# A decoder layer on one core: the remaining transposes, those of the softmax among them, through VectorE blocks and DRAM, and attention five steps earlier

## Chip, cores and metric

One core of a Trainium2 chip runs the whole layer. The metric is device time in microseconds: three runs of the kernel before gave 2067.03 to 2070.13 us, median 2067.54. TensorE is PE in the rows, VectorE DVE, ScalarE ACT, GpSimd POOL, and SyncE SP, whose queue issues all DMAs here.

## What is computed

A layer over 256 positions of width 2048, all float32:

```
x = x + 1/2 * SwiGLU_1(rms(x))                      # D_FF 5632
h = rms(x);  q|k|v|u|v_sg|g_att|g_sg = h @ w_in     # 12 heads of 128 in 3 groups, u and v_sg 1536 wide
y_att = (attention of the 3 groups, weighted by their softmax denominators) @ w_att_out
y_sg  = (gelu(u) * (tril(sg_w) @ LN(gelu(v_sg)) + sg_b)) @ w_sg_out
x = x + (sigmoid(g_att) * y_att + sigmoid(g_sg) * y_sg) @ w_out
x = x + 1/2 * SwiGLU_2(rms(x));  out = rms(x)
```

The three groups have dilations 1, 4 and 16. Attention works on four slots; a slot is one head of each group, and its softmax runs over the three groups at once (1152 columns of scores for 128 rows: 384 for the first row block, 768 for the second).

## The kernel before

Each weight gemm makes 512 output columns for both row blocks of 128 positions. Its weights come as units of four k-tiles (512 rows x 512 columns, 1 MiB, tile `raw`, three buffers). A unit has two *steps*; a step is two k-tiles. For a step, ScalarE rounds the weights to `wh` (L131) and VectorE makes the rest `wl` (L132), and TensorE does 12 matmuls (L146 to L148: hi x wh, hi x wl, lo x wh, for two k-tiles and two row blocks). Splits are issued `LA` = 3 steps ahead of the products, into four buffers. All 776 steps stand in one list `hus` in the order of the calls of `gemm`; the loop at the end (L747 on) goes through it, issues the products of a step, then the callbacks that `at(i, fn)` put at it, then the loads and splits that are due. Nothing else sets the order of work. Each engine takes its instructions in that order, and SP's queue too.

The left operand of a gemm must lie transposed (model dimension on partitions), in two parts hi and lo. There are two ways to turn it. Either TensorE transposes 128x128 pieces into a bank of the tag `tp`, and ScalarE and VectorE empty it; or `turn` (L158): at step i VectorE transposes 32x32 blocks (L165) into `bt` and SP writes it to DRAM (`bm`, L168, 512 KB); at step i+3 SP reads it back in four parts of 32 partitions (L174); at step i+6 ScalarE and VectorE make hi and lo. The h of both feed-forward blocks, q and k, c = 0 to 2 of the two inner norms and c = 0 to 2 of the merge go through `turn`. TensorE still transposes: x for the first norm while it is loaded, c = 3 of the norms (`norm_transposes`, L208) and of the merge (L612), the spatial weights (L343), the gated u (L421), the softmax (L519, L522) and the attention output (L555).

A feed-forward block runs in two halves of 6 and 5 column blocks of h. The gate and up gemms have 8 steps each, a down gemm 12 steps in the first half and 10 in the second; four down gemms follow each half. The last h of a half is turned while the first down gemm runs. Its callbacks, with e the last step of the up gemm: multiply e+1, blocks e+2, read e+5, evacuation e+8; the first down gemm reaches that h at step e+9 of the second half (e+11 of the first).

Mixer: v_sg, u, then q and k of each group, then v, then four times (gate of the spatial branch, `w_sg_out`, gate of attention, `w_att_out`), then `w_out`. `spatial(e)` puts its product, gate, transposes and evacuation for six pairs of groups at steps e to e+8. `attention(e)` puts slot s at e0 = e + 5s: scores e0, softmax e0+1, transposes e0+3, evacuation e0+4, p@v e0+5, normalisation, transposes and evacuation of the output up to e0+8.

Of the kernel before, what the change touches and what calls it, by code (L numbers as in the profile page):

```python
# [8 lines left out]
F32 = mybir.dt.float32  # L9
# [3 lines left out]
OP = mybir.AluOpType  # L13
# [28 lines left out]
def layer(ctx: ExitStack, tc: tile.TileContext, a, out):  # L42
# [58 lines left out]
    def gemm(w, c0, rows0, nk, lhs, post, before=None):  # L101
        g = dict(w=w, c0=c0, rows0=rows0, nk=nk, lhs=lhs, post=post)
        gemms.append(g)
        for u in range(nk // UK):
            for j in range(2):
                hus.append((g, u, j))
# [51 lines left out]
    def turn(i, name, src, dst, ev):  # L158
        got = {}

        def blocks():
            d = sb.tile([P, 4, 4, NT, 32], F32, tag="gate", bufs=2, name=f"bt{name}")
            v = src()
            for t in range(NT):
                DVE.transpose(d.rearrange("p j k t b -> p t k j b")[:, t],  # L165
                              v[:, t].rearrange("p (k j b) -> p k j b", j=4, b=32))
            m = got["m"] = dram.tile([P, 4, S], F32, tag="turn", name=f"bm{name}")
            SP.dma_start(m, d.rearrange("p j k t b -> p j (k t b)"))  # L168

        def back():  # L170
            got["e"] = e = dst()
            m = got["m"].rearrange("(i a) j r -> j a i r", a=32)
            for j in range(4):
                SP.dma_start(e[32 * j:32 * j + 32].rearrange("p t c -> p (t c)").rearrange("p (i r) -> p i r", i=4),  # L174
                             m[j])

        at(i, blocks)
        at(i + 3, back)
        at(i + 6, lambda: ev(got["e"].rearrange("p t c -> p (t c)").rearrange("p (i q b) -> p q i b", i=4, b=32)))

    def turned(ap):
        return ap.rearrange("p k (t i b) -> p (k t) i b", t=NT, b=32)

# [34 lines left out]
    def residual(e, n, c, banks, scale, norm):  # L218
# [14 lines left out]
        if c < 3:  # L233
            def evac(src):
                for j in range(4):
                    v = src[:, 2 * j:2 * j + 2]
                    k = 16 * n + 4 * c + j
                    ACT.activation(v, v, AF.Copy, scale=gcols[:, k:k + 1])
                ks = slice(4 * c, 4 * c + 4)
                split_psum(turned(xT["hi"][:, ks]), turned(xT["lo"][:, ks]), src)  # L240

            turn(e + 2, f"x{n}_{c}", lambda: x[:, :, cs],
                 lambda: sb.tile([P, NT, NC], F32, tag="gate", bufs=2, name=f"xt{n}_{c}"), evac)
            return
        got = {}

        def tr():
            for kk in range(2):
                ks = [4 * c + 2 * kk, 4 * c + 2 * kk + 1]
                got[kk] = ks, norm_transposes(f"{n}_{ks[0]}", ks)  # L250
            if c == 3:
                norm_rstd(n)

        def ev():
            for kk in range(2):
                norm_evac(n, *got[kk])

        at(e + 2, tr)
        at(e + 3, ev)


    def ffn(wg, wu, wd, down_post):
        halves = ((0, 6), (6, 11))
        for hf, (f0, f1) in enumerate(halves):
# [8 lines left out]
            for f in range(f0, f1):  # L273
# [10 lines left out]
                def post_up(e, banks, st=st, f=f, f0=f0):  # L284
# [17 lines left out]
                    turn(e + 2, f"h{e}", lambda: sg, lambda: sg, ev)  # L302

                gemm(wg, f * NC, 0, KD, lhs_x, post_gate)
                gemm(wu, f * NC, 0, KD, lhs_x, post_up)
            for c in range(4):
                gemm(wd, c * NC, f0 * NC, 4 * (f1 - f0), lhs_h,
                     lambda e, banks, c=c, hf=hf: down_post(e, c, banks, hf == 1))
# [5 lines left out]
    ffn(a["ffn1_w_gate"][0], a["ffn1_w_up"][0], a["ffn1_w_down"][0], down1)  # L314
# [12 lines left out]
    def mixer_consts():  # L327
        SP.dma_start(cs_t, a["rope_cs"])
        SP.dma_start(mask, a["att_mask"])
        raw = big.tile([P, NG, P], F32, tag="C", name="sgw")  # L330
        SP.dma_start(raw, a["sg_w"][0].rearrange("g t s -> t g s"))
        mix["sgraw"] = raw
# [7 lines left out]
    def sgw_transposes(q):  # L340
        b = tp_bank(f"sgw{q}").rearrange("p (j s) -> p j s", j=4)
        for j in range(4):
            PE.transpose(b[:, j], mix["sgraw"][:, 4 * q + j], ident)  # L343
        mix["sgwb", q] = b

    def sgw_evac(q):
        ACT.activation(mix["wspT"][:, 4 * q:4 * q + 4], mix["sgwb", q], AF.Copy)
        if q == 2:
            POOL.affine_select(mix["wspT"], mix["wspT"], pattern=[[0, NG], [1, P]], compare_op=OP.is_ge,
                               fill=0.0, base=0, channel_multiplier=-1)  # L350
# [44 lines left out]
    def spatial(e):  # L395
        for pg in range(6):
# [19 lines left out]
            def tr(pg=pg, got=got):  # L416
                b = tp_bank(f"spt{pg}").rearrange("p (j s) -> p j s", j=2)
                for j in range(2):
                    g = 2 * pg + j
                    for t in range(NT):  # L420
                        PE.transpose(b[:, j, t * P:(t + 1) * P], mix["u"][:, t, g * P:(g + 1) * P], ident)  # L421
                got["t"] = b

            def ev(pg=pg, got=got):
                g = slice(2 * pg, 2 * pg + 2)
                split_psum(mix["uT"][:, 0, g], mix["uT"][:, 1, g], got["t"])

            at(e + pg, prod)
            at(e + pg + 1, gate)
            at(e + pg + 2, tr)  # L430
            at(e + pg + 3, ev)

    def post_qk(key, gi):
        def post(e, banks):
# [5 lines left out]
            def flat(v):  # L440
# [370 lines left out]
```

## Time and profile before

| | |
|---|---|
| median of three runs | 2067.54 us (2067.03 to 2070.13) |
| the profiled execution | 2066.57 us, its span 2064.8 us |
| granted TensorE clock | 0.999 |
| TensorE busy, loading weights | 99%, 87% |
| VectorE, ScalarE, GpSimd busy | 56%, 47%, 0% |
| DMA | 455 MB, the dynamic queue's packets 68.1% of 16 engines' span |

A row of a view groups instructions by source line and tile; `out<-in` names the tiles. "Idle before" is the time for which the engine stood still ahead of an instruction, and the name behind it is what ended that. A matmul's own duration overlaps the next one's; how fast TensorE goes is read from the starts.

### The profile page before, as it was taken

The page shows a single profiled execution, that of the slowest core. Times are in us where ns is not written, and L with a number is a line of the kernel's source. Part 1 is how long each engine was busy: PE and PEld are TensorE (multiplying, and loading weights), DVE is VectorE, ACT ScalarE, POOL GpSimd, SP SyncE. Part 2 cuts the span into 40 slices and gives each one's busy share as a digit, 9 for nine tenths or more (in the row PEclk, how much of TensorE's full clock was granted, in tenths as well). Part 3 has the DMA queues.
Part 4 walks back from the last instruction along what each step waited for, and adds up shares of the span by engine and source line. Part 5 has one row for each costly group of instructions (what it writes and reads, how often), then busy time and mean ns, then how long its engine had stood idle before and what let it go on. Part 6 is the DMA issues. An engine that isn't in the chain of part 4 may idle for free.

```text
span 2064.8 us, 23874 instructions
## 1 busy us (share of the span) xinstructions
PE 2051.4 (99%) x9601; PEld 1794.1 (87%) x9601; DVE 1164.2 (56%) x1172; ACT 970.8 (47%) x1071; POOL 9.4 (0%) x13
## 2 busy tenths in 40 slices
PE   9999999999999999999999999999999999999998
PEld 7888888888888888888888888888888888888887
DVE  5555555455555555665555555665555555555554
ACT  6444444444445544444455444554444444444443
POOL 0000000000000000000000000000000000000000
PEclk9999999999999999999999999999999999999999
DMA  7777776677786666578646666676677766677764
GB/s 266 234 234 224 224 224 204 204 223 225 243 277 225 224 204 204 192 245 260 200 143 207 223 221 206 222 246 223 223 233 233 223 202 202 222 224 242 234 209 142
DMA packets 237399, 455.20 MB, mean 220 GB/s; under 512 B 9644, under 2 KB 32360, under 8 KB 237160
## 3 DMA queue, kind: packets, MB, share of 16 engines
q1 hardware_dynamic: 237288, 453.68, 68.1%
q8 instruction: 75, 1.23, 0.2%
q14 instruction: 36, 0.29, 0.0%
HBM read 432.14 MB, written 21.50 MB: 220 GB/s over the span
## 4 chain that ended last, share of the span: by engine, by line
PE 98%; DMA 1%; DVE 0%; issue 0%; ACT 0%; SPq 0%; ACTq 0%; POOLq 0%; POOL 0%; DVEq 0%
PE mm L148 32%; PE mm L147 32%; PE mm L146 32%; DMA bmh<-bth 0%; DMA raw<-in_ffn_w_gate_dram 0%; PE sc L495 0%; PE sp L405 0%; DMA sg<-bmh 0%; ACT wh L131 0%; PE pv L543 0%; PE pv L542 0%; PE pv L538 0%; PE sc L493 0%; PE spt L421 0%; PE pt L522 0%
## 5 line engine op out<-in xcount | busy, mean ns | idle before, releaser
L132 DVE TENSOR_TENSOR wl<-raw,wh 128x1024 fp32r<-128x1024 f32 (+1 forms) x777 | 948.6, 1223 | 855.9 <-ACT wh L131 851.3
L131 ACT ACTIVATE wh<-raw 128x1024 fp32r<-128x1024 f32 (+1 forms) x777 | 817.8, 1055 | 1023.1 <-PE mm L148 1013.0
L146 PE MATMUL mm<-wh,xhi 128*128 128x512 f32 x2144 | 815.9, 381 | 0.0
L147 PE MATMUL mm<-wl,xhi 128*128 128x512 f32 x2144 | 813.1, 379 | 0.7 <-DVE wl L132 0.7
L148 PE MATMUL mm<-wh,xlo 128*128 128x512 f32 x2144 | 812.6, 379 | 0.0
L147 PEld LDWEIGHTS mm<-wl,xhi 128*128 128x128 f32 x2144 | 405.2, 189 | 58.9 <-DVE wl L132 1.8
L148 PEld LDWEIGHTS mm<-wh,xlo 128*128 128x128 f32 x2144 | 405.2, 189 | 57.3
L146 PEld LDWEIGHTS mm<-wh,xhi 128*128 128x128 f32 x2144 | 405.2, 189 | 57.1
L148 PE MATMUL mm<-wh,hlo 128*128 128x512 f32 x704 | 267.0, 379 | 1.1 <-DVE hlo L154 1.1
L146 PE MATMUL mm<-wh,hhi 128*128 128x512 f32 x704 | 267.1, 379 | 0.0
L147 PE MATMUL mm<-wl,hhi 128*128 128x512 f32 x704 | 266.8, 379 | 0.0
L148 PEld LDWEIGHTS mm<-wh,hlo 128*128 128x128 f32 x704 | 133.1, 189 | 20.8 <-DVE hlo L154 1.9
L146 PEld LDWEIGHTS mm<-wh,hhi 128*128 128x128 f32 x704 | 133.1, 189 | 18.9 <-ACT hhi L153 0.2
L147 PEld LDWEIGHTS mm<-wl,hhi 128*128 128x128 f32 x704 | 133.1, 189 | 18.8
L146 PE MATMUL mm<-wh,mhi 128*128 128x512 f32 x128 | 48.6, 380 | 0.0
L147 PE MATMUL mm<-wl,mhi 128*128 128x512 f32 x128 | 48.5, 379 | 0.0
L148 PE MATMUL mm<-wh,mlo 128*128 128x512 f32 x128 | 48.5, 379 | 0.0
L146 PE MATMUL mm<-wh,uT 128*128 128x512 f32 x96 | 36.7, 383 | 0.0
L147 PE MATMUL mm<-wl,uT 128*128 128x512 f32 x96 | 36.4, 379 | 0.0
L148 PE MATMUL mm<-wh,uT 128*128 128x512 f32 x96 | 36.4, 379 | 0.0
L294 DVE SCALAR_TENSOR_TENSOR sg<-mm,rstd,sg 128x512 f32<-128x512 f32 x44 | 30.9, 744 | 0.0
L194 ACT ACTIVATE junk<-x 128x512 bf16<-128x512 f32 x30 | 18.9, 629 | 21.9 <-DVE x L223 15.7
(144 smaller groups left out, 644.1 us busy)
## 6 DMA issues: line engine op xcount, KB each, us to landing
raw<-in_w_in_dram SPq DMA_DIRECT2D x92, 1024.0 KB, 5.0
raw<-in_ffn_w_up_dram SPq DMA_DIRECT2D x88, 1024.0 KB, 5.2
raw<-in_ffn_w_down_dram SPq DMA_DIRECT2D x88, 1024.0 KB, 5.0
raw<-in_ffn_w_gate_dram SPq DMA_DIRECT2D x85, 1024.0 KB, 5.1
raw<-in_w_out_dram SPq DMA_DIRECT2D x16, 1024.0 KB, 5.2
raw<-in_w_sg_out_dram SPq DMA_DIRECT2D x12, 1024.0 KB, 5.5
bmh<-bth SPq DMA_DIRECT2D x22, 512.0 KB, 3.3
sg<-bmh SPq DMA_DIRECT2D x88, 128.0 KB, 4.9
```

The lines of the kernel that those rows point to most:

```text
L131: ACT.activation(wh[:, k], r[:, k], AF.Copy)
L132: DVE.tensor_tensor(wl[:, k], r[:, k], wh[:, k].bitcast(F32), op=OP.subtract)
L146: PE.matmul(o, hi[:, k, tt], in_turn(wh[:, jj]), start=first, stop=False)
L147: PE.matmul(o, hi[:, k, tt], in_turn(wl[:, jj]), start=False, stop=False)
L148: PE.matmul(o, lo[:, k, tt], in_turn(wh[:, jj]), start=False, stop=last)
L194: ACT.activation(junk, x[:, t, c * NC:(c + 1) * NC], AF.Square, accum_out=ss[n][:, t, c:c + 1])
L294: DVE.scalar_tensor_tensor(two(sg[:, t]), banks[t], rstd[:, t:t + 1], two(sg[:, t]), op0=OP.mult, op1=OP.mult)
```

## The change

It takes the last transposes in the middle of the program from TensorE and gives them to `turn`, which is made general: `put` fills the blocks (`put_tokens` for a token-major tile, `put_flat` for columns as they lie), and q 32-column blocks a row are moved.

- Norms 1 and 2: c = 3 goes through `turn` too; c = 1 begins four steps later (e+6).
- Merge: c = 3 goes through `turn`.
- Spatial weights: two turns of six groups each, 30 and 22 steps ahead of the end of the first feed-forward block, in a tile `room` of 4096 columns that takes the place of `sgw`.
- Spatial branch: three turns of four groups each, blocks at e+3, e+5, e+7, read back into `room`.
- Softmax: one turn of 1152 columns a slot, blocks e0+3, read e0+6, evacuation e0+9, so p@v is at e0+10 and the output's evacuation at e0+13. `attention` is called with e+16 in place of e+21.
- Pairs: two neighbouring gemms can be laid out so that all units but the last of both come first, then the last of the first, then the last of the second. Paired are the first two down gemms of each half, the first two of v_sg, of `w_out`, and the first gate and up of the second feed-forward block.

```diff
-    def gemm(w, c0, rows0, nk, lhs, post, before=None):
...
+    def gemm(w, c0, rows0, nk, lhs, post, pair=False):
+        gemms.append(dict(w=w, c0=c0, rows0=rows0, nk=nk, lhs=lhs, post=post, pair=pair))
+    def lay_out():
+        i = 0
+        while i < len(gemms):
+            gs = gemms[i:i + 2] if gemms[i]["pair"] else gemms[i:i + 1]
+            i += len(gs)
+            units = [(g, u) for g in gs for u in range(g["nk"] // UK)]
+            if len(gs) == 2:
+                units.sort(key=lambda q: q[1] == q[0]["nk"] // UK - 1)
+            for g, u in units:
+                hus.extend([(g, u, 0), (g, u, 1)])
...
-    def turn(i, name, src, dst, ev):
+    def turn(i, name, q, put, dst, ev):
         def blocks():
-            d = sb.tile([P, 4, 4, NT, 32], F32, tag="gate", bufs=2, name=f"bt{name}")
...
+            d = sb.tile([P, 4, q, 32], F32, tag="gate", bufs=2, name=f"bt{name}")
+            put(d)
+            m = got["m"] = dram.tile([P, 4, q * 32], F32, tag="turn", name=f"bm{name}")
+            SP.dma_start(m, d.rearrange("p j m b -> p j (m b)"))
...
+    def put_tokens(src):
+        def put(d):
+            v = src()
+            for t in range(NT):
+                DVE.transpose(d.rearrange("p j (k t) b -> p t k j b", t=NT)[:, t],
+                              v[:, t].rearrange("p (k j b) -> p k j b", j=4, b=32))
+        return put
+    def put_flat(src):
+        def put(d):
+            DVE.transpose(d.rearrange("p j m b -> p m j b"), src().rearrange("p (m j b) -> p m j b", j=4, b=32))
+        return put
...
+        turn(e + (6 if c == 1 else 2), f"x{n}_{c}", 8, put_tokens(lambda: x[:, :, cs]),
+             lambda: flat(sb.tile([P, NT, NC], F32, tag="gate", bufs=2, name=f"xt{n}_{c}")), evac)
...
+        turn(i, f"w{h}", 6, put_flat(lambda: mix["room"][:, part]), lambda: mix["room"][:, part], ev)
...
-            at(e + pg + 2, tr)
-            at(e + pg + 3, ev)
+        for r in range(3):
...
+            turn(e + 3 + 2 * r, f"u{r}", 8, put_tokens(lambda r=r: mix["u"][:, :, r * NC:(r + 1) * NC]),
+                 lambda r=r: mix["room"][:, (1536, 2560, 0)[r]:(1536, 2560, 0)[r] + 2 * NC], ev)
...
-                attention(e + 21)
+                attention(e + 16)
...
+            def ev(src, s=s, got=got):
+                pT = sb.tile([P, 9, P], F32, tag="L", bufs=2, name=f"pT{s}")
+                ACT.activation(in_blocks(pT[:, 0:5]), src[:, 0:5], AF.Copy)
+                DVE.tensor_copy(in_blocks(pT[:, 5:9]), src[:, 5:9])
...
-            for k, f in ((0, qk), (1, softmax), (3, tr), (4, ev), (5, pv), (6, nrm), (7, otr), (8, oev)):
+            for k, f in ((0, qk), (1, softmax), (10, pv), (11, nrm), (12, otr), (13, oev)):
                 at(e0 + k, f)
+            turn(e0 + 3, f"p{s}", 9, put_flat(lambda got=got: got["p"]), lambda got=got: got["p"], ev)
...
+            turn(e + 2, f"m{c}", 8, put_tokens(lambda: ga), lambda: flat(ga),
...
+    lay_out()
+    for h in range(2):
+        sgw_turn(ffn_hus - 30 + 8 * h, h)
```

Three places show how instructions move. The first is TensorE where the down gemms of the second half reach the last h. A row is a matmul; `mm224` is the first down gemm, `mm234` before and `mm232` now the second, `wh232` the split of step 232. Before:

```order
L148 MATMUL mm224_0_4266<-wh231_4348,hlo159_3093 128x512
L146 MATMUL mm224_1_4267<-wh231_4348,hhi159_3092 128x512
L147 MATMUL mm224_1_4267<-wl231_4349,hhi159_3092 128x512
L148 MATMUL mm224_1_4267<-wh231_4348,hlo159_3093 128x512
L146 MATMUL mm224_0_4266<-wh232_4370,hhi159_3092 128x512
L147 MATMUL mm224_0_4266<-wl232_4371,hhi159_3092 128x512
L148 MATMUL mm224_0_4266<-wh232_4370,hlo159_3093 128x512
```

Now:

```order
L154 MATMUL mm232_1_4427<-wh239_4496,hhi159_3092 128x512
L155 MATMUL mm232_1_4427<-wl239_4497,hhi159_3092 128x512
L156 MATMUL mm232_1_4427<-wh239_4496,hlo159_3093 128x512
L154 MATMUL mm224_0_4266<-wh240_4514,hhi159_3092 128x512
L155 MATMUL mm224_0_4266<-wl240_4515,hhi159_3092 128x512
L156 MATMUL mm224_0_4266<-wh240_4514,hlo159_3093 128x512
```

The last unit of `mm224`, which reads the last h, stood at step 232 and stands at step 240; eight steps of the second gemm lie ahead of it.

The second is TensorE between two steps of the mixer, at the softmax of the first slot (`pt` its transposes, `p0` the softmax). Before:

```order
L148 MATMUL mm376_1_7278<-wh383_7345,xlo1_4477 128x512
L519 MATMUL pt0_0_7433<-ident_76,p0_7388 128x128
L522 MATMUL pt0_1_7434<-ident_76,p0_7388 128x128
L522 MATMUL pt0_2_7435<-ident_76,p0_7388 128x128
L519 MATMUL pt0_0_7433<-ident_76,p0_7388 128x128
L522 MATMUL pt0_1_7434<-ident_76,p0_7388 128x128
```

These and the other transposes of the list above are gone from TensorE's queue; in their place SP's queue has, for this slot:

```order
L173 DMA bmp0_7338<-btp0_7336 128x1152
L179 DMA p0_7289<-bmp0_7338 32x4x288 x4
```

The third is SP's queue from the spatial branch (`u`) on into the turn of the first q; `raw` are weight loads. Before:

```order
L122 DMA raw161_6009<-in_w_in_dram 128x4x512
L122 DMA raw162_6065<-in_w_in_dram 128x4x512
L122 DMA raw163_6123<-in_w_in_dram 128x4x512
L122 DMA raw164_6179<-in_w_in_dram 128x4x512
L168 DMA bmq0_6228<-btq0_6225 128x1024
L122 DMA raw165_6230<-in_w_in_dram 128x4x512
L122 DMA raw166_6264<-in_w_in_dram 128x4x512
L174 DMA q0_6141<-bmq0_6228 32x4x256 x4
```

Now:

```order
L173 DMA bmu0_6054<-btu0_6051 128x1024
L130 DMA raw162_6056<-in_w_in_dram 128x4x512
L173 DMA bmu1_6103<-btu1_6100 128x1024
L130 DMA raw163_6105<-in_w_in_dram 128x4x512
L179 DMA room_4282<-bmu0_6054 32x4x256 x4
L173 DMA bmu2_6152<-btu2_6149 128x1024
L130 DMA raw164_6156<-in_w_in_dram 128x4x512
L179 DMA room_4282<-bmu1_6103 32x4x256 x4
L173 DMA bmq0_6209<-btq0_6206 128x1024
L130 DMA raw165_6211<-in_w_in_dram 128x4x512
L179 DMA room_4282<-bmu2_6152 32x4x256 x4
L130 DMA raw166_6251<-in_w_in_dram 128x4x512
```

Three writes and three groups of reads now stand among the weight loads 162 to 166, ahead of the first q's read.

## Rows read from the trace of the kernel before

**Rows 1.** The profile page, its first part (busy time, share of the span and instructions of each engine) and its fourth (the chain of work that ended last, share of the span by engine).

```profile
PE 2051.4 (99%) x9601; PEld 1794.1 (87%) x9601; DVE 1164.2 (56%) x1172; ACT 970.8 (47%) x1071; POOL 9.4 (0%) x13
PE 98%; DMA 1%; DVE 0%; issue 0%; ACT 0%; SPq 0%; ACTq 0%; POOLq 0%; POOL 0%; DVEq 0%
```

**Rows 2.** The two rows of TensorE's waits that concern the product matmuls: line, what it waited for, us in total, times, longest.

```profile
PE mm L148 <- DVE hlo L154: 1.1, 2, 0.6
PE mm L147 <- DVE wl L132: 0.7, 1, 0.7
```

**Rows 3.** Stretches of the span: us, busy us (and instructions) of each engine, granted TensorE clock, share of the DMA engines, GB/s. The first two hold the loads of the mixer's constants and one turn, 830 to 860 the spatial branch; 905 to 920 lies among the turns of q and k.

```profile
590.00:600.00 10.00, 10.00 (x48) 8.77 (x47) 7.43 (x8) 3.87 (x5) 0.00 (x0) 1.00 0.98 354
600.00:610.00 10.00, 10.00 (x48) 8.77 (x47) 4.90 (x4) 4.09 (x4) 0.00 (x0) 1.00 1.01 340
830.00:845.00 15.00, 15.00 (x77) 13.17 (x76) 9.55 (x15) 5.68 (x7) 0.00 (x0) 1.00 0.43 141
845.00:860.00 15.00, 15.00 (x77) 13.17 (x76) 11.10 (x22) 7.44 (x10) 0.00 (x0) 1.00 0.42 140
...
905.00:920.00 15.00, 15.00 (x71) 13.15 (x70) 7.94 (x10) 7.99 (x9) 0.00 (x0) 1.00 1.00 323
```

**Rows 4.** Two groups of VectorE's instructions (count, busy us, mean ns of one, idle before), two splits in ScalarE's order of time (start us, us, what ended the idle time before), and two rows of the waits of all engines (total us, times, longest).

```profile
L132 DVE TENSOR_TENSOR wl<-raw,wh 128x1024 fp32r<-128x1024 f32 x775 | 947.2, 1224 | 855.0 <-ACT wh L131 850.4
L165 DVE STREAM_TRANSPOSE bth<-sg 128x512 f32<-128x512 f32 x44 | 28.5, 687 | 0.0
...
1954.13 1.06 ACT L131 ACTIVATE wh<-raw 128x1024 fp32r<-128x1024 f32 x1 [1.53 <-PE mm L148]
1956.72 1.06 ACT L131 ACTIVATE wh<-raw 128x1024 fp32r<-128x1024 f32 x1 [1.53 <-PE mm L148]
...
ACT wh L131 <- PE mm L148: 1013.0, 707, 3.5
ACT qkT L461 <- DMA k<-bmk: 5.2, 3, 1.9
```

**Rows 5.** Groups of TensorE's instructions with their shapes kept apart: count, then busy us and mean ns of one, then idle time before.

```profile
L522 PE MATMUL pt<-ident,p 128*128 128x128 f32 x24 | 4.1, 272 | 0.0
L421 PE MATMUL spt<-ident,uv 128*128 128x128 f32 x24 | 3.6, 273 | 0.0
L519 PE MATMUL pt<-ident,p 128*128 128x128 f32 x12 | 3.3, 272 | 0.0
L208 PE MATMUL xt<-ident,x 128*128 128x128 f32 x16 | 2.1, 273 | 0.0
L343 PE MATMUL sgw<-ident,sgw 128*128 128x128 f32 x12 | 1.8, 273 | 0.0
L612 PE MATMUL mt<-ident,ga 128*128 128x128 f32 x8 | 1.0, 273 | 0.0
```

**Rows 6.** TensorE in order of time where the first four transposes of the spatial weights stand between two steps: start us, us, instruction, count.

```profile
646.95 0.38 PE L148 MATMUL mm<-wh,hlo 128*128 128x512 f32 x1
647.17 0.60 PE L343 MATMUL sgw<-ident,sgw 128*128 128x128 f32 x4
...
647.82 0.38 PE L147 MATMUL mm<-wl,hhi 128*128 128x512 f32 x1
648.04 0.38 PE L148 MATMUL mm<-wh,hlo 128*128 128x512 f32 x1
```

**Rows 7.** TensorE in order of time at the softmax transposes of the first slot.

```profile
1018.94 0.38 PE L148 MATMUL mm<-wh,xlo 128*128 128x512 f32 x1
1019.15 0.27 PE L519 MATMUL pt<-ident,p 128*128 128x128 f32 x1
...
1020.35 0.38 PE L147 MATMUL mm<-wl,xhi 128*128 128x512 f32 x1
```

**Rows 8.** TensorE in order of time at its two waits for the last part of h, in the second half of each feed-forward block; the bracket gives the idle time before and its releaser.

```profile
612.89 0.38 PE L147 MATMUL mm<-wl,hhi 128*128 128x512 f32 x1
613.83 0.48 PE L148 MATMUL mm<-wh,hlo 128*128 128x512 f32 x1 [0.56 <-DVE hlo L154]
614.15 0.38 PE L146 MATMUL mm<-wh,hhi 128*128 128x512 f32 x1
...
1972.28 0.38 PE L147 MATMUL mm<-wl,hhi 128*128 128x512 f32 x1
1973.17 0.48 PE L148 MATMUL mm<-wh,hlo 128*128 128x512 f32 x1 [0.52 <-DVE hlo L154]
```

**Rows 9.** DMA issues: out<-in, queue, count, KB each, median us from issue to landing.

```profile
raw<-in_w_in_dram SPq DMA_DIRECT2D x92, 1024.0 KB, 5.0
bmh<-bth SPq DMA_DIRECT2D x22, 512.0 KB, 3.3
sg<-bmh SPq DMA_DIRECT2D x88, 128.0 KB, 4.9
k<-bmk SPq DMA_DIRECT2D x12, 128.0 KB, 8.5
```

**Rows 10.** Two waits of SP's queue (total us, times, longest), and the weight load that SP issued between 924.6 and 927 us (KB, us to landing).

```profile
SPq L168 <- DVE btk L165: 22.0, 3, 8.4
SPq L174 <- DMA bmh<-bth: 36.9, 22, 6.3
...
raw<-in_w_in_dram SPq DMA_DIRECT2D x1, 1024.0 KB, 8.4
```

More of the change, by code (lines that the diff above doesn't have):

```diff
@@ L232, in residual, with evac, ffn @@
             return
[L233 to L262, printed above, removed]
+        if c == 3:
+            at(e + 2, lambda: norm_rstd(n))
+        def evac(src):
+            for j in range(4):
+                v = src[:, 2 * j:2 * j + 2]
+                k = 16 * n + 4 * c + j
+                ACT.activation(v, v, AF.Copy, scale=gcols[:, k:k + 1])
+            ks = slice(4 * c, 4 * c + 4)
+            split_psum(turned(xT["hi"][:, ks]), turned(xT["lo"][:, ks]), src)
+        turn(e + (6 if c == 1 else 2), f"x{n}_{c}", 8, put_tokens(lambda: x[:, :, cs]),
+             lambda: flat(sb.tile([P, NT, NC], F32, tag="gate", bufs=2, name=f"xt{n}_{c}")), evac)
+    def ffn(wg, wu, wd, down_post, pair):
         halves = ((0, 6), (6, 11))
@@ L301, in post_up @@
                     at(e + 1, mul)
-                    turn(e + 2, f"h{e}", lambda: sg, lambda: sg, ev)
-                gemm(wg, f * NC, 0, KD, lhs_x, post_gate)
+                    turn(e + 2, f"h{e}", 8, put_tokens(lambda: sg), lambda: flat(sg), ev)
+                gemm(wg, f * NC, 0, KD, lhs_x, post_gate, pair and f == 0)
                 gemm(wu, f * NC, 0, KD, lhs_x, post_up)
@@ L338, in mixer_consts, with sgw_turn, ev @@
             SP.dma_start(mix[nm], bass.AP(tensor=v.tensor, offset=v.offset, ap=[[0, P], [1, SGW]]))
[L340 to L350, printed above, removed]
+    def sgw_turn(i, h):
+        part = slice(768 * h, 768 * h + 768)
+        def ev(src):
+            ACT.activation(in_blocks(mix["wspT"][:, 6 * h:6 * h + 6]), src, AF.Copy)
+            if h == 1:
+                POOL.affine_select(mix["wspT"], mix["wspT"], pattern=[[0, NG], [1, P]], compare_op=OP.is_ge,
+                                   fill=0.0, base=0, channel_multiplier=-1)
+        turn(i, f"w{h}", 6, put_flat(lambda: mix["room"][:, part]), lambda: mix["room"][:, part], ev)
     def post_gelu(key, j):
@@ L414, in gate, with ev @@
                                              op0=OP.add, op1=OP.mult)
[L416 to L426, printed above, removed]
             at(e + pg, prod)
             at(e + pg + 1, gate)
-            at(e + pg + 2, tr)
-            at(e + pg + 3, ev)
+        for r in range(3):
+            def ev(src, r=r):
+                g = slice(4 * r, 4 * r + 4)
+                split_psum(turned(mix["uT"][:, 0, g]), turned(mix["uT"][:, 1, g]), src)
+            turn(e + 3 + 2 * r, f"u{r}", 8, put_tokens(lambda r=r: mix["u"][:, :, r * NC:(r + 1) * NC]),
+                 lambda r=r: mix["room"][:, (1536, 2560, 0)[r]:(1536, 2560, 0)[r] + 2 * NC], ev)
     def post_qk(key, gi):
@@ L599, in post @@
             at(e + 1, add)
[L600 to L621 removed]
+            turn(e + 2, f"m{c}", 8, put_tokens(lambda: ga), lambda: flat(ga),
+                 lambda src: split_psum(turned(mix["mhi"][:, 4 * c:4 * c + 4]),
+                                        turned(mix["mlo"][:, 4 * c:4 * c + 4]), src))
         return post
     for j in range(3):
[L625 removed]
+        gemm(w_in, o_s + j * NC, 0, KD, lhs_x, post_gelu("vs", j), j == 0)
     for j in range(3):
@@ L639, in layer @@
         gemm(a["w_out"][0], c * NC, 0, KD, lambda: (mix["mhi"], mix["mlo"]),
-             lambda e, banks, c=c: residual(e, 2, c, banks, 1.0, True))
+             lambda e, banks, c=c: residual(e, 2, c, banks, 1.0, True), c == 0)
     fin = {}
@@ L695, in layer @@
     at(11 * 16 + 24 + 24, mixer_consts)
-    for q in range(3):
-        at(ffn_hus - 20 + q, lambda q=q: sgw_transposes(q))
-        at(ffn_hus - 19 + q, lambda q=q: sgw_evac(q))
+    for h in range(2):
+        sgw_turn(ffn_hus - 30 + 8 * h, h)
     at(n - 60, load_fin)
```

80 lines of the change are left out of this document (17 added, 63 removed).

## Prediction

> **What bounds the kernel now.** I read the page's busy shares and its chain of waits first: TensorE is busy for 99% of the span and carries 98% of the chain, while VectorE is at 56% and ScalarE at 47% [rows 1]. Next I asked for TensorE's waits, to see whether anything still holds it. The product matmuls wait 1.1 us on a late last part of h, twice, and 0.7 us on the first weights [rows 2]. So a TensorE instruction that goes shortens the kernel by the time it takes in the sequence, and work that moves to VectorE, ScalarE or the DMA queues is free until it makes TensorE wait. [...]
>
> The cover is thick on the splits. One step (12 matmuls) takes 2.59 us, the distance of two splits on ScalarE, and its split costs 1.06 us there and 1.22 on VectorE; ScalarE stood still 1013 us in all because it had to wait for TensorE to give a split's buffer back [rows 4]. Splits run three steps ahead, 7.8 us.
>
> **What leaves TensorE.** 96 transposes: 36 of the softmax (24 + 12), 24 of the spatial branch, 16 of the two norms, 12 of the spatial weights, 8 of the merge [rows 5]. Their price is not the mean of 272 to 273 ns in that view, which is the time one is in the pipeline. It is what they push the next matmul back. From the matmul at 646.95 to the second one behind four transposes are 0.87 us; two steps of the sequence without them take 0.43 (0.22 each, 647.82 to 648.04), so four cost 0.44 or 0.110 each [rows 6]. Behind nine softmax transposes it is 1.41 - 0.43 = 0.98, or 0.109 each [rows 7]. 60 x 0.110 + 36 x 0.109 = **10.5 us off the path**.
> [...]
>
> **What the pairs give back.** In the second half of each feed-forward block the first down product needs the last h at its ninth step, one step behind that turn's evacuation. TensorE lost 613.83 - 612.89 = 0.94 against 0.22, and 0.10 more up to the next matmul: 0.8 us; at 1972.28 to 1973.17 it is 0.89 against 0.22, again 0.8 with the same tail [rows 8]. Paired, the need comes eight steps (20.7 us) later, and that wait goes: **1.6 us**. All four product banks are then taken, but the first gemm of a pair ends two steps (5.2 us) before its banks are wanted and they are emptied right after it: no cost. What is late next there is the third turn of a norm or of the merge. Its evacuation follows step e+8 and its first reader is step e+13, four whole steps or 10.4 us of cover, against 3.3 + 4.9 us of median landings in the whole turn [rows 9]. Nothing waits.
>
> **What is added, off the path.** Twelve turns: two of norms, one of the merge, three of the spatial branch, two of the spatial weights, four of the softmax. VectorE's block transposes cost 2 x 0.687 us for 1024 columns [rows 4], so six x 1.37 = 8.2; scaled by columns, 1.03 for each half of the spatial weights and 1.55 for a slot's 1152 columns: 8.3 more. That is 16.5 us over the span, at most 1.55 in one step, where 2.59 - 1.22 = 1.37 is open and the three steps of lead take the rest. The evacuations replace others of like size. Attention starts five steps sooner and each slot is five steps longer, so its last evacuation stays where it was, three steps ahead of its reader. A slot's p@v follows its turn by 7 steps (18 us) against landings of 3.3 and, at the slowest row, 8.5 us: covered by 6 us. The spatial weights are turned more than 60 steps before their reader: no cost.
>
> **What may come back.** A turn moves 0.5 MB out and 0.5 MB in through the queue that also loads the weights. Most of the twelve fall where there is room. The three of the spatial branch do not: they start two steps apart and run straight into the turns of q and k, every eight steps. In SP's order five weight loads, four writes and four groups of reads stand from the first write of u to the last read of q0: 5.24 + 2.10 + 2.10 = 9.4 MB. With turns among them the engines moved 323 GB/s at a share of 1.00, and 340 and 354 in the crowded 20 us from 590 [rows 3]; at 323 that is 29 us of work. The stretch lasts 12 steps, 31.1 us, plus two groups of spatial matmuls. It was at 0.42 to 0.43 [rows 3] and becomes about nine tenths full, with each transfer behind another. Behind it the turns of k already land in 8.5 us and ScalarE waits up to 1.9 us for them [rows 4, 9], so a backlog is worked off slowly. The trace has one such place: the crowd from 590 us on, where a turn came late and TensorE lost 0.8 us [rows 3, 8].
> [...]
>
> So I bound the price of a late turn by nothing and by the 0.8 us of the one measured, and take 0.8 us for the three turns of u and the next three of q and k that inherit the queue: **4.8 us given back**. Bounds: 0 (all hidden, as 22 turns of h but two are) and 12 x 0.8 = 9.6 (each new turn as late as that one).
>
> **Sum.** The profiled execution took 2066.57 us (span 2064.8 and 1.8 around it). 2066.57 - 10.5 - 1.6 + 4.8 = 2059.3. The median of the runs is 2067.54, 0.97 above it: **2060.3 us**. What a measurement of this kernel can tell from no change is about 0.2%, or 4.1 us: 2063.4 and below is faster, above 2071.7 slower.
>
> **Rivals.**
> 1. *Everything is hidden.* For it: TensorE is busy for the whole of each stretch shown from 830 to 920 us, at a DMA share up to 1.00 [rows 3]. Against it: that part of the program has one turn at a time. 2067.54 - 12.1 = 2055.4.
> 2. *Each new turn comes late*, in the norms and the softmax too. 2055.4 + 9.6 = 2065.0, which counts as the same.
> 3. *Slower: the weights run dry.* SP issues in order. A turn's write waits for VectorE, up to 8.4 us, and its read for the write, up to 6.3; the weight load behind them then needs up to 8.4 to land [rows 10]. A buffer is free five steps (12.9 us) ahead of its split, and the split three steps (7.8) ahead of TensorE: it decides at 20.7 us. One hold and a landing are 16.8, which is why the q and k turns cost nothing now. With a write and a read of neighbouring turns between two loads, as in the spatial branch, 8.4 + 6.3 + 8.4 = 23.1, or 2.4 us of TensorE's time for each load so caught. Slower takes over 16.2 us, seven loads; with eight, 2055.4 + 19.2 = 2074.6. Against it: only two or three loads stand so, and the longest holds don't fall together.
> 4. *The transposes cost their duration.* 96 x 0.273 = 26.2 in place of 10.5: 2060.3 - 15.7 = 2044.6. Rows 6 and 7 speak against it; it would need a cost that the next matmul's start doesn't show.
>
> **How the numbers follow.** Forecast with 2.4 to 7.2 given back, 2057.8 to 2062.6 and what lies between it and 2063.4: 0.53. Rival 1: 0.24. Rival 2 with what lies around it: 0.15. Rival 3: 0.06. Rival 4: 0.02. Faster is the forecast, rivals 1 and 4: 0.79; the same is rival 2, 0.15; slower is rival 3, 0.06. The range runs from just under rival 1 (2054.5) to rival 2 with the scatter of a run (2065.5) and leaves out rivals 3, 4 and the upper edge of 2: under 0.2.
>
> **What would show it.** The 96 transposes and nothing else gone from TensorE's rows, and its busy time less by some 10 us. No wait on hlo in the second halves. In the spatial stretch a DMA share near 0.9, ScalarE waiting for the reads of u and for weights, and TensorE with a handful of waits of under 1 us on wh or wl from there to the last turn of k, 3 to 7 us in all. No wait of p@v. If TensorE shows no waits there, rival 1 was right; waits of several us on weights, with SP's queue holding on a turn ahead of each, are rival 3; waits in the norms and at p@v are rival 2.

## The result, and the profile after

The changed kernel takes 2057.32 us in the median of six runs (2055.02 to 2058.62) against 2067.48 for six runs of the kernel before: a ratio of 0.9946, 95% interval 0.9935 to 0.9957, or 10.2 us faster. Its profiled execution took 2058.14 us, with a span of 2056.4. The forecast was 2060.3 in a range of 2054.5 to 2065.5. In all that follows one run is left out: one of kernel 2 of the experiments took 4599 us, more than twice any other.

First the page of the changed kernel, its busy times and its chain; they answer to [rows 1].

```profile
PE 2043.6 (99%) x9505; PEld 1785.7 (87%) x9505; DVE 1173.7 (57%) x1180; ACT 968.0 (47%) x1062; POOL 7.0 (0%) x13
...
PE 95%; DMA 2%; DVE 1%; issue 1%; ACT 0%; SPq 0%; ACTq 0%; POOLq 0%; POOL 0%; DVEq 0%
```

TensorE has 9505 instructions in place of 9601: the 96 transposes and nothing else. Its busy time is less by 7.8 us, not by the 10 that were to show it (by 9.4 in kernel 3 below, which loses nothing). The other engines hardly differ (VectorE +9.5 us, ScalarE -2.8). In the chain DMA goes from 1% to 2% and TensorE from 98% to 95%: somewhere the end was set by transfers.

The waits of TensorE's matmuls, and then of its weight loads, changed kernel (line, what it waited for, us in total, times, longest); they answer to [rows 2].

```profile
PE mm L155 <- DVE wl L140: 1.0, 2, 0.8
PE mm L154 <- ACT wh L139: 0.2, 1, 0.2
...
PEld mm L155 <- DVE wl L140: 4.0, 9, 1.1
PEld mm L154 <- ACT wh L139: 0.6, 1, 0.6
```

The wait on hlo is gone, no wait of p@v has come, and there are short waits on the splits. Read from the matmuls alone they look like 1.2 us, read from the weight loads like 4.6; neither is what TensorE lost. A surer measure is when each step begins. Below, every product matmul of the program is counted in steps of twelve, and the start of a step in the changed kernel is set against the same step before. Only changes of the difference count; its first value, 0.82, is from the kernel's head and stands from step 7 on (30.29 us against 29.47). Steps 373 to 399 are not shown, since attention's matmuls stand five steps earlier there and shift the difference for a while.

```
step   before    after    after - before, and what lies ahead of it
 232   612.62   613.43   +0.82
 240   634.22   634.15   -0.07   first wait on hlo                     -0.88
 248   656.26   654.87   -1.38   12 transposes, spatial weights        -1.32
 272   719.29   717.03   -2.26   8 transposes, first norm              -0.88
 322   856.61   851.71   -4.89   24 transposes, spatial branch         -2.63
 328   872.15   867.25   -4.89
 336   892.87   889.87   -3.00   LOST                                  +1.90
 344   913.59   911.02   -2.56   LOST                                  +0.43
 352   934.31   932.64   -1.67   LOST                                  +0.89
 372   986.11   984.44   -1.67
 400  1077.12  1071.51   -5.61   36 transposes, softmax                -3.94
 500  1339.23  1332.74   -6.48   8 transposes, merge                   -0.88
 520  1391.90  1384.54   -7.36   8 transposes, second norm             -0.88
 760  2014.29  2006.14   -8.15   second wait on hlo                    -0.79
```

The transposes give 1.32 + 0.88 + 2.63 + 3.94 + 0.88 + 0.88 = 10.53 us, the pairs 1.67, and 3.22 us are lost in one stretch of 65 us, behind the spatial branch. Stretches of it in the changed kernel, with the columns of [rows 3]:

```profile
845.00:860.00 15.00, 15.00 (x71) 13.12 (x70) 12.58 (x21) 7.49 (x8) 0.00 (x0) 1.00 1.01 308
860.00:875.00 15.00, 15.00 (x71) 13.15 (x70) 6.99 (x6) 5.90 (x6) 0.00 (x0) 1.00 1.07 277
875.00:890.00 15.00, 13.90 (x62) 11.30 (x61) 10.22 (x17) 7.68 (x9) 0.00 (x0) 1.00 0.60 208
```

The kernel before had a share of 0.42 in the first of these stretches [rows 3], but in the second, which [rows 3] leaves out, it was already at 0.87:

```profile
860.00:875.00 15.00, 15.00 (x72) 13.12 (x71) 8.45 (x9) 7.34 (x10) 0.00 (x0) 1.00 0.87 280
```

Now the DMA engines are full for 30 us, and TensorE falls short only after that, when they are no longer full. The clock stays at 1.00. TensorE at the first gap (start us, us, instruction, idle before and releaser):

```profile
877.40 0.38 PE L156 MATMUL mm<-wh,xlo 128*128 128x512 f32 x1
877.97 0.48 PE L154 MATMUL mm<-wh,xhi 128*128 128x512 f32 x1 [0.20 <-ACT wh L139]
879.23 0.48 PE L155 MATMUL mm<-wl,xhi 128*128 128x512 f32 x1 [0.78 <-DVE wl L140]
879.55 0.38 PE L156 MATMUL mm<-wh,xlo 128*128 128x512 f32 x1
```

Starts lie 0.57, 1.26 and 0.32 apart instead of 0.22. The cause is read one engine further back. ScalarE in order of time, the same kernel:

```profile
861.25 1.06 ACT L161 ACTIVATE uT<-room 128x1024 fp32r<-128x1024 f32 x1 [3.10 <-DMA room<-bmu]
...
868.80 1.06 ACT L161 ACTIVATE uT<-room 128x1024 fp32r<-128x1024 f32 x1 [4.61 <-DMA room<-bmu]
869.77 1.99 ACT L139 ACTIVATE wh<-raw 128x1024 fp32r<-128x1024 f32 x2
875.19 0.63 ACT L462 ACTIVATE qkT<-q 128x512 f32<-128x512 f32 x1 [3.43 <-DMA q<-bmq]
875.73 1.25 ACT L446 ACTIVATE k<-mm,rstd 128x512 f32<-128x512 f32 x2
876.87 3.89 ACT L139 ACTIVATE wh<-raw 128x1024 fp32r<-128x1024 f32 x4
...
890.56 2.00 ACT L139 ACTIVATE wh<-raw 128x1024 fp32r<-128x1024 f32 x2 [4.61 <-DMA raw<-in_w_in_dram]
```

And SP's queue at the same time (start us, us from there to the end of the row's last issue, transfer, count):

```profile
862.27 5.08 SPq L179 DMA_DIRECT2D q<-bmq  x4
867.66 6.15 SPq L130 DMA_DIRECT2D raw<-in_w_in_dram  x2
883.40 0.34 SPq L173 DMA_DIRECT2D bmk<-btk  x1
883.84 2.17 SPq L130 DMA_DIRECT2D raw<-in_w_in_dram  x2
```

These two views together show a loop. The reads of u and of the first q land late, so ScalarE stands still, for 3.10, 4.61 and 3.43 us, and only then does four splits in a row (876.87). The copy of k out of PSUM stands behind the same stall (875.73), so VectorE's blocks of k are late, and SP waits for them until 883.40 with the next weight load behind that write. No weight load is issued between 873.8 and 883.84; the one of 883.84 lands at 890.45, and at 890.56 ScalarE begins its split, after a wait of 4.61 us. The turn of k, too, begins late. Two landings of the changed kernel (KB each, median us), and two waits of SP's queue, which answer to [rows 9, 10]:

```profile
room<-bmu SPq DMA_DIRECT2D x12, 128.0 KB, 7.6
q<-bmq SPq DMA_DIRECT2D x12, 128.0 KB, 8.1
```

```profile
SPq L173 <- DVE btk L189: 30.3, 3, 10.5
SPq L179 <- DMA bmh<-bth: 31.9, 22, 6.2
```

The longest hold of SP on k's blocks grew from 8.4 to 10.5 us; its waits ahead of the reads of h are as before. The medians of the landings say little by themselves: q's reads took 7.0 us before, and 7.7 in kernel 3 below, which loses nothing. It is the first q that is late: its reads are issued from 862.27 us on, and the last lands at 875.09.

### The profile page after: what moved, and what is told of

It reads as the page before. It is cut to its first block, busy times and chain, and to the rows that moved or that the text cites. A ratio compares the mean times of both kernels' runs of the same rounds, so it can differ in the third digit from the quotient of the medians.

```text
span 2056.4 us, 23813 instructions
## 1 busy us (share of the span) xinstructions
PE 2043.6 (99%) x9505; PEld 1785.7 (87%) x9505; DVE 1173.7 (57%) x1180; ACT 968.0 (47%) x1062; POOL 7.0 (0%) x13
## 4 chain that ended last, share of the span: by engine, by line
PE 95%; DMA 2%; DVE 1%; issue 1%; ACT 0%; SPq 0%; ACTq 0%; POOLq 0%; POOL 0%; DVEq 0%
PE mm L155 31%; PE mm L154 31%; PE mm L156 31%; DMA q<-bmq 1%; DMA room<-bmu 1%; DMA k<-bmk 0%; DVE wl L140 0%; PE sc L496 0%; DMA x<-in_x_dram 0%; SPq L179 0%; ACT wh L139 0%; PE xtf L231 0%; PE sp L413 0%; DMA bmq<-btq 0%; DMA bmk<-btk 0%
```

## The experiments

All kernels but the first differ from the changed kernel by the edit shown, with `...` for what is left out. "Lost" is always the delay of steps 328 to 372 in the table's sense, in the profiled execution. Kernels 1 to 4 ran on one chip, 5 to 8 on a second, 9 and 10 on a third; the kernel before, run beside them, took 2067.40, 2067.54 and 2067.66 us there. The ratios are to these.

**1. The change again.** No edit.

> The changed kernel itself, beside the next three on the same chip. It ran at 2057.32 us in the median (2055.0 to 2058.6), 10.2 us below the kernel before. Every theory expects 2055.5 to 2058.5 here. The profiled run of it started its steps 330 to 352 (877 to 925 us) 3.2 us later than its lead over the kernel before at step 322: if that is of the mechanism and not of that one run, the same stretch loses 2 to 4 us again, in gaps of 0.5 to 1.3 us in front of single products.

Measured: 2057.16 us (2054.57 to 2060.46; ratio 0.995, 0.9937 to 0.9962). The profiled execution, that of 2060.46 us, lost 5.3 us: 3.27 up to step 336, then 0.59, 0.78 and 0.70. So the loss is of the kernel and not of one run, it lies in the same stretch, and its size changes from run to run. Taken over the eleven runs of this program, the times go from 2054.6 to 2060.5.

**2. Less crowd: u's transposes back on TensorE.**

```
-            turn(e + 3 + 2 * r, f"u{r}", 8, put_tokens(...), ...)
...
+            at(e + pg + 2, tr)
+            at(e + pg + 3, ev)
```

`tr` has four transposes for each pair of groups, and `ev` their evacuation, both as in the kernel before.

> The spatial branch's 24 transposes stand on TensorE again, as in the kernel before; all else is as in the change. On TensorE that costs 24 x 0.11 = 2.6 us. Theory (the three turns of u crowd the queue, and what is late behind them, from 877 to 925 us, is their doing): the gaps of steps 330 to 352 go, 2 to 3.2 us come back, and the sum is the change plus 2.6 - (2 to 3.2), or 2056.5 to 2058. Rival (the turns of q and k, or the loads, are late there whatever u does): the gaps stay and the time is the change plus 2.6, some 2060. A third reading, that nothing was lost there and the run of after was only a slow one, gives 2060 with no gaps in this stretch in either kernel.

Measured: 2057.26 us, four runs from 2057.07 to 2057.71 (ratio 0.995, 0.9937 to 0.9964). Lost: 0.00. The DMA share is 0.42 and then 0.91, much as in the kernel before (0.42 and 0.87). SP still waits up to 8.8 and 9.0 us for the blocks of k and q; without the crowd these holds cost nothing.

```profile
845.00:860.00 15.00, 15.00 (x75) 13.16 (x74) 11.43 (x20) 7.77 (x11) 0.00 (x0) 1.00 0.42 149
860.00:875.00 15.00, 15.00 (x72) 13.12 (x71) 7.96 (x9) 7.36 (x10) 0.00 (x0) 1.00 0.91 290
```

```profile
SPq L173 <- DVE btk L189: 23.7, 3, 8.8
```

**3. The same crowd, stretched: u's reads spread.**

```
...
-        at(i + 3, back)
-        at(i + 6, lambda: ev(...))
+        at(i + 3 + wait, back)
+        at(i + 6 + wait, lambda: ev(...))
...
+                 wait=(0, 8, 14)[r], tag="turnu", bufs=3)
```

> The turns of u are written as in the change, but into three DRAM buffers of their own, and their reads are issued 0, 8 and 14 steps later, so that they fall into the gaps between the turns of q and k. Nothing is added or taken away in work or bytes. Theory (crowding of reads and weight loads in one stretch): the gaps of steps 330 to 352 go, and the time falls by 2 to 3.2 us, to 2054 to 2055.5. Rival (SP holds the weight loads behind a turn's write that waits for VectorE, so the turns of q and k stay late by themselves): at most 1 us of it comes back, 2056.3 to 2057.5.

Measured: 2054.79 us, five runs from 2054.76 to 2054.95 (ratio 0.9938, 0.9925 to 0.9952). Lost: 0.00. Stretches of this kernel:

```profile
860.00:875.00 15.00, 15.00 (x71) 13.15 (x70) 7.65 (x12) 7.39 (x9) 0.00 (x0) 1.00 1.02 320
875.00:890.00 15.00, 15.00 (x71) 13.12 (x71) 10.87 (x13) 7.32 (x7) 0.00 (x0) 1.00 0.84 252
```

The share is at 1.02 here too, and SP's holds are nearly as long as in the change:

```profile
SPq L173 <- DVE btk L189: 25.3, 3, 9.9
```

So this kernel does not free the DMA engines; it takes two groups of u's reads out from ahead of q's. TensorE is busy throughout. Still ScalarE waits 16.1 us for raw weights (six times, 3.5 us at most), against 22.1 (4.9 at most) in the changed kernel; TensorE loses nothing by it.

**4. The same crowd, short holds: each write one step later.**

```
-            SP.dma_start(m, d.rearrange("p j m b -> p j (m b)"))
+            got["d"] = d
+        def write():
+            SP.dma_start(got["m"], got["d"].rearrange("p j m b -> p j (m b)"))
...
+        at(i + 1, write)
```

> The write of every turn to DRAM is issued one step (2.6 us) later in SP's order than VectorE's blocks, so that it finds them made and the weight load behind it isn't held; reads stay where they are. Theory (SP's holds on a turn's write, up to 10.5 us in the trace of after, make the raw weights late for ScalarE): the waits of the splits on raw weights (22.1 us in 6 after the change) fall to a third or less, the gaps of steps 336 to 352 go, and the time falls by 1.5 to 3 us, to 2054.5 to 2056. Rival (the DMA engines have more to move in this stretch than time): the holds turn into late landings, the gaps stay, the time is the same within 1 us. A third case: a turn's data arrive 2.6 us later everywhere, and the tightest of the feed-forward turns lose 0.5 to 1 us each, which makes it slower.

Measured: 2054.79 us, five runs from 2054.60 to 2055.09 (ratio 0.9938, 0.9926 to 0.9951). Lost: 0.10. SP's longest hold on a write of k falls from 10.5 to 0.8 us. A part of the holds moves to the reads, which now wait for the write, up to 4.3 us for one of u's:

```profile
SPq L176 <- DVE btk L193: 2.5, 3, 0.8
SPq L182 <- DMA bmu<-btu: 6.3, 2, 4.3
```

ScalarE's wait for raw weights of the mixer falls to 5.3 us, a quarter. A stretch of this kernel, and SP's queue:

```profile
860.00:875.00 15.00, 15.00 (x71) 13.12 (x71) 6.75 (x8) 7.36 (x10) 0.00 (x0) 1.00 0.99 317
```

```profile
865.13 1.74 SPq L182 DMA_DIRECT2D q<-bmq  x4
866.97 12.57 SPq L130 DMA_DIRECT2D raw<-in_w_in_dram  x3
880.38 0.34 SPq L176 DMA_DIRECT2D bmk<-btk  x1
882.63 0.37 SPq L130 DMA_DIRECT2D raw<-in_w_in_dram  x1
```

Between q's reads and k's write three weight loads go out instead of two, and k's write is 3 us earlier. The third of these loads is the one that stood behind k's write in the change: it is issued at 879.17 us instead of 883.84 and lands at 884.89 instead of 890.45. The reads of u and q land sooner than in the change, but the writes land later (6.0 and 5.8 us in place of 3.0), so that a turn's two transfers together take about as long:

```profile
bmu<-btu SPq DMA_DIRECT2D x3, 512.0 KB, 6.0
room<-bmu SPq DMA_DIRECT2D x12, 128.0 KB, 5.5
q<-bmq SPq DMA_DIRECT2D x12, 128.0 KB, 5.5
```

Kernels 2 to 4 each take away one half: long holds without u's reads ahead of q's lose nothing (2 and 3), u's reads in place with short holds lose 0.1 us (4), and both together, in the change, lose 0 to 6 us.

**5. Softmax transposes back on TensorE**, on top of kernel 3, with attention at its former place.

```
-                attention(e + 16)
+                attention(e + 21)
...
-            for k, f in ((0, qk), (1, softmax), (10, pv), ...
+            for k, f in ((0, qk), (1, softmax), (3, tr), (4, ev), (5, pv), ...
...
```

> The kernel with u's reads spread (2054.79 us, five runs within 0.2) with one part of the change undone: the softmax's 36 transposes stand on TensorE again, and attention begins where it did before, five steps later, with its former offsets. Nothing else differs, and the base has no waits that a shift could hide. Theory (a transpose costs TensorE the 0.109 us by which it pushes the next matmul back, and each slot's waits are covered): 36 x 0.109 = 3.9 us, so 2058.7. Rival (it costs its 273 ns in the pipeline): 36 x 0.273 = 9.8, so 2064.6. Rival (the gain came from the shorter slots or the earlier start, not from the transposes): under 2 us, below 2056.8.

Measured: 2059.97 us (2059.49 to 2060.62; ratio 0.9963, 0.9949 to 0.9976), 5.2 above kernel 3 where 3.9 was expected. The steps say where: across attention the difference to kernel 3 is 3.94 us, or 36 x 0.109. Another 0.92 is at the second norm, which no edit touched. There ScalarE stood still for a turn of the norm, and TensorE has a gap a little later:

```profile
1366.20 1.71 ACT L263 ACTIVATE xt<-xt,gcols 128x256 f32<-128x256 f32 x4 [2.93 <-DMA xt<-bmx]
```

```profile
1374.72 0.38 PE L154 MATMUL mm<-wh,xhi 128*128 128x512 f32 x1
1375.76 0.48 PE L155 MATMUL mm<-wl,xhi 128*128 128x512 f32 x1 [0.65 <-DVE wl L140]
```

It is the same kind of loss (0.9 us at a turn, behind 15 us with a DMA share of 1.04), in a place that was clean in every other trace but that of kernel 9. The 0.3 us that remain are not placed. So the price of a transpose is settled, and the expectation's "no waits that a shift could hide" was too sure. Kernel 3 has the same norm, with a share of 1.02, and loses nothing there; what tipped it here is not shown.

**6. No pairs of down gemms**, on top of kernel 3.

```
-   lambda e, banks, c=c, hf=hf: down_post(e, c, banks, hf == 1), c == 0)
+   lambda e, banks, c=c, hf=hf: down_post(e, c, banks, hf == 1), False)
```

> The kernel with u's reads spread with the other part undone: no down gemm is paired with the next, so that the last part of h is needed at the ninth step of each second half again. Theory (a late turn of h costs TensorE 0.8 us in each of two blocks): 1.6 us, so 2056.4, with two gaps of about 0.9 us between product matmuls, one in each second half. Rival (the pairs move the wait elsewhere or give nothing): 2054.8.

Measured: 2056.88 us (2056.34 to 2057.26; ratio 0.9948, 0.9934 to 0.9961), 2.1 above kernel 3; the profiled execution is the one of 2056.34. In it the wait on h is back:

```profile
PE mm L156 <- DVE hlo L162: 1.1, 2, 0.6
```

The steps give 0.83 us in the first block and 0.79 in the second, 1.6 in all. What the other runs have on top, up to 0.9 us, no trace shows.

**7. Only ScalarE's stall on u taken away: u's evacuations three steps later.**

```
-        at(i + 6, lambda: ev(...))
+        at(i + 6 + late, lambda: ev(...))
```

`late` is 3 for the turns of u and 0 for all others.

> The change with one shift: the evacuations of u's three turns stand three steps (7.8 us) later in ScalarE's and VectorE's order. Every transfer, every hold of SP's queue and every byte is as in the change. It tells which link of the chain does the damage. Theory A (ScalarE, which works in order, stands still for late reads of u, 3.1 to 5.3 us at a time, and the splits behind it fall back; from then on the loads are late too): the gaps at 872 to 885 us go, and with them those that follow; 2054.8 to 2055.5. Theory B (the weight loads are late by themselves, from SP's holds and the full queue, and ScalarE's stalls on u only fall into that wait): the raw waits and the gaps stay, 2056 to 2058.5 with the scatter of the change.

Measured: 2059.52 us (2056.95 to 2061.26; ratio 0.9959, 0.9946 to 0.9971), no better than the change, whose eleven runs its five overlap. ScalarE in its profiled execution, that of 2056.95 us, which lost 2.5 us:

```profile
860.16 1.04 ACT L161 ACTIVATE uT<-room 128x1024 fp32r<-128x1024 f32 x1
...
865.31 1.06 ACT L139 ACTIVATE wh<-raw 128x1024 fp32r<-128x1024 f32 x1 [2.46 <-DMA raw<-in_w_in_dram]
...
873.93 0.63 ACT L462 ACTIVATE qkT<-q 128x512 f32<-128x512 f32 x1 [5.67 <-DMA q<-bmq]
```

Theory A has fallen. ScalarE no longer waits for u, and it waits as long for raw weights (23.7 us in all, 22.1 in the change) and for q (13.6 and 11.5). The loss does not need the stall on u; the stalls on raw weights and on the first q are there without it.

The traces can be lined up along this link. In the change and in kernels 7, 4 and 3 step 330 begins within half a us of the same time. ScalarE begins on the first q at 875.19, 873.93, 872.17 and 869.85 us; the weight load that follows k's write in the change is issued at 883.84, 883.71, 879.17 and 878.50; and 3.22, 2.52, 0.10 and 0.00 us are lost.

**8. Turns issued by GpSimd.** In `turn`, `SP.dma_start` becomes `POOL.dma_start`, at the write and at the four reads.

> The change with the writes and reads of all turns issued by GpSimd instead of SP: places, bytes and buffers are the same, but a turn's write that waits for VectorE, or its read that waits for the write, no longer stands ahead of a weight load. Theory (order in one queue): SP's holds on turns are gone, weight loads go out when their buffer is free, TensorE has no gaps from 877 to 925 us, 2054.5 to 2055.5. Rival (bytes in the stretch): weights then compete with the turns' reads, which land later, and ScalarE waits for q, k and u as before or more: 2056 to 2060. A third case, in which GpSimd's small tasks (the norms' powers) now stand behind its own holds: a wait of the norms' first readers of up to some us, 2056 to 2059, with no gaps at 877 to 925.

Measured: 2082.73 us (2081.23 to 2085.71; ratio 1.0073, 1.0059 to 1.0086): slower by 15 us than the kernel before, above the range of every expectation. SP's holds are gone as meant, but the turns themselves became slower: the writes of q and k land in 6.2 and 4.8 us in the median, where they took 3.0. GpSimd's time to issue, and ScalarE's waits on the turns of q and k:

```profile
L179 POOL DMA_DIRECT2D k<-bmk x12 | 6.6, 554 | 14.9 <-DMA bmk<-btk 10.0 <-ACT wh L139 4.9
```

```profile
ACT qkT L462 <- DMA k<-bmk: 22.3, 3, 8.2
ACT qkT L462 <- DMA q<-bmq: 20.0, 3, 9.9
```

A read takes 0.55 us to issue, against a median of 0.43 on SP in the change, and ScalarE waits 42.3 us for q and k where it waited 23.6. The loss is spread: 11 us around the first norm (steps 248 to 280), 18 from step 328 to 372. The edit also changes more than the order: the page lists 51.40 MB of this kernel's packets under another kind of queue, `software_dynamic`; the pages of the kernel before, of the change and of kernels 3, 4 and 9 have none of it. The experiment therefore does not isolate SP's order, and kernel 4 remains the evidence for that. Nor were the bytes moved faster: in stretches of 15 us from 830 to 935 us the rate was at most 299 GB/s, against 320 in kernel 3.

**9. The reads cut the other way.**

```
-            m = got["m"].rearrange("(i a) j r -> j a i r", a=32)
-            for j in range(4):
-                SP.dma_start(e[32 * j:32 * j + 32].rearrange(...), m[j])
+            m = got["m"].rearrange("(i a) j r -> i j a r", a=32)
+            ei = e.rearrange("p (i r) -> p i r", i=4)
+            for i in range(4):
+                SP.dma_start(ei[:, i], m[i])
```

> The change with another cut of each turn's read: four transfers of 128 KB as before, of the same 1 KB pieces, at the same place, but each goes to all 128 partitions instead of one to each group of 32. Holds, order and bytes are as in the change. Where the queue stood full from 845 to 875 us, the change moved 240 to 336 GB/s in stretches of 5 us. Theory (the rate at which the crowd drains decides whether the loads are late, and a read that is confined to 32 partitions drains slowly): the reads of u and q land in 5 to 6 us instead of 8, the gaps from 877 to 925 us go, 2054.6 to 2055.5, and the runs scatter by a few tenths. Rival (the four reads are in flight together and cover all partitions anyway; the order of SP's queue decides): landings and gaps stay, 2055 to 2060, as in the change.

Measured: 2111.15 us (2107.29 to 2112.31; ratio 1.0206, 1.0192 to 1.022): slower by 43 us than the kernel before, against both theories. TensorE's waits, and how long SP took to issue one read of u (min, median, max ns):

```profile
PE mm L154 <- ACT wh L139: 20.9, 12, 3.6
PE mm L155 <- DVE wl L140: 14.1, 16, 2.2
```

```profile
L180 SPq DMA_DIRECT2D room<-bmu x12: 622/1108/2914, 857.5 to 880.2; - x12
```

In the changed kernel these were 313, 480 and 1150 ns. SP itself is occupied by the reads (6.65 and 7.73 us for two groups of four), while the DMA share from 850 to 885 us is only 0.37 to 0.89 in stretches of 5 us, so the DMA engines were not full there. The weight loads behind them are late again and again. What makes this cut so costly is not shown: its landings are missing from the trace. By the theory, the author's guess that a read confined to 32 partitions drains slowly, the cut across all 128 would be the faster one. Here it is the slower one, by 54 us (2111.15 against 2057.16). As SP's issue differs too, no run tests that guess by itself.

**10. Both mends.** Kernels 3 and 4 together.

> The change with both mends: u's reads spread over the gaps between the turns of q and k, and every turn's write issued one step later. Each alone gave 2054.79 us with no gap of TensorE from 845 to 930 us. Theory (what the change gave back is all recovered by either, and 10.5 + 1.6 us are what there is): 2054.6 to 2055.0, the same as either alone, with runs within some tenths. Rival (each mend left a part that the other would free): below 2054.4.

Measured: 2054.70 us (2054.48 to 2055.09; ratio 0.9936, 0.9924 to 0.9949), nothing lost. It is the same as either alone, and 2.6 us better than the change. Its steps gain 12.2 us from 232 to 760, which is all of 10.53 + 1.67.

## Why the prediction was right, and where its size was off

- **The transposes: right.** 10.53 us by the steps, 10.5 predicted. Kernel 5 puts 36 of them back and pays 3.94 across attention, 0.109 each. Rival 4, the 273 ns each, is out.
- **The pairs: right.** 1.67 us predicted as 1.6, and kernel 6 loses 1.6 when they go. The third turn of a norm cost nothing in the change, as predicted; kernel 5 shows one case where a turn of the norm did cost 0.9 us.
- **The added turns of the norms, the merge, the weights and the softmax: right.** The differences in the table change there by the transposes alone, and no wait of p@v appears. Rival 2 is out.
- **The crowd behind the spatial branch: the place right, the mechanism half named, the size too large.** I took 6 turns x 0.8 = 4.8 us. The profiled execution gave back 3.22, that of the first experiment 5.3; against the 2054.8 us of the kernels that lose nothing, the median run gives back 2.5, and the eleven runs go from 0 to 5.7. The step that failed is the count: u's own three turns cost TensorE nothing (steps 322 to 328), and the loss is in the three turns behind them, with 1.90, 0.43 and 0.89 us. These three had been named as those that inherit the queue, and rightly; that u's turns cost as much was wrong, since u's readers are far off and only ScalarE stands still, and kernel 7, without that, loses 2.5 us all the same. The price of 0.8 us, from one turn of the feed-forward block, was wrong the other way: in the profiled execution three turns lost 3.22, or 1.07 each. That a count too high and a price too low partly made up for each other is luck. Of the 3.0 us by which the forecast was too high, 2.3 are this term.
- **Why there is a loss: the rate was put too high and the holds were set aside.** The 29 us of transfers in 31.1 were worked out at 323 GB/s, with a share near 0.9 to follow; the trace shows 1.01 and 1.07, at 308 and 277 GB/s. At their mean, 292, the 9.4 MB are an estimated 32 us of work, as long as the stretch itself. Nor was the whole stretch at 0.42 to 0.43 before, as I read it: from 860 us on it was at 0.87. I gave rival 3, SP's order, 0.06 because its full size needs seven loads. In small it is half of the mechanism: shorten the holds (kernel 4) or take u's reads out of the way (kernels 2 and 3), and the loss is gone.
- **Rival 1, everything hidden** (2055.4), is what kernels 3, 4 and 10 reach, at 2054.7 to 2054.8. The 0.6 us between are no more than the 0.97 by which I set the median of before above the execution that the sum was made in.

Open: what decides in one run whether the change loses 0 or 6 us. The loop above can carry a delay from one turn to the next, so a small difference in landing could decide it, but this is not shown: the two traced executions took 2058.14 and 2060.46 us, and none of the change that lost nothing was traced. Nor is it shown why the writes of kernel 4 land later and its reads sooner.

## What to carry to other kernels

Price an instruction on the bounding engine by how far it pushes the next one back (0.109 us a transpose here, with a duration of 0.273), and check the price afterwards by lining up the starts of the same steps in both traces; the list of the matmuls' waits showed 1.2 of the 3.2 us lost. In a queue that issues in the order of the program, as SP's did here, put a transfer that waits for a computation after that computation is done, not at the place where it is begun: one step of delay for the writes was worth as much here as moving two groups of reads out of the crowded stretch (2054.79 us either way). A full share of the DMA engines is not itself a loss (kernels 3 and 4 have it, at 1.02 and 0.99, and lose 0.1 us at most); ask which load stands behind what when it is full.

## What the runs showed of the hardware that was not expected

- A higher share of the DMA engines was not a higher rate: from 860 to 875 us they moved 277 GB/s at 1.07 in the change, but 320 at 1.02 and 317 at 0.99 in kernels 3 and 4, whose transfers as a whole are the same, in another order.
- The time that SP takes to issue one transfer is not fixed: one read of u took at most 0.52 us in kernel 4, 1.15 in the change and 2.91 in kernel 9. A full share doesn't explain it, since kernel 4 has one (0.99) and kernel 9 has not.
- The cut of a 512 KB read into four, by partitions or across them, decided over 50 us of the kernel (2057 against 2111).
- In one stretch of kernel 9, in which TensorE was busy for 9.57 of 15 us, its granted clock was 0.83 in the mean. It was 1.00 in the 15 us ahead and 0.94 in the 15 us behind, with TensorE busy throughout in both. From 880 to 885 us, where TensorE was busy for only 2.34 of 5 us, it was 1.00. What the lower clock cost is not separated from the waits:

```profile
660.00:675.00 15.00, 9.57 (x39) 7.58 (x38) 6.72 (x7) 7.35 (x10) 1.48 (x1) 0.83 0.69 202
```
